# An encoder trunk on one core: pooled product after the keys, output products two gates behind, two reciprocal roots on GpSimd, first squares on ScalarE

## The chip, the core and the metric

The kernel runs on one core of a Trainium2 chip. TensorE (PE) multiplies matrices and writes to PSUM; VectorE (DVE), ScalarE (ACT) and GpSimd (POOL) do the elementwise work; SyncE (SP) issues nearly all DMAs. The metric is the device time of one execution in microseconds, taken as the median of several runs.

## The reference

Two layers of an encoder on x of 512 tokens by 1024 channels, in float32. Cut to what matters:

```python
h = rms_norm(x, attn_norm_g[l])
proj = h @ w_in[l]
c_q, c_kv, k_rope, gq, gk, gv, pool_in, gate_logits = split_columns(proj, IN_SIZES)
o_mla = mla_branch(c_q, c_kv, k_rope, ...)    # 8 heads, low rank; per-head RMS norm of q and k (96 wide), rotary part
o_gqa = gqa_branch(gq, gk, gv, ...)           # 8 heads over 2 key heads; per-head RMS norm (64 wide), rotary
o_pool = pool_branch(pool_in, pool_w[l], pool_scale[l])   # centred means over 2, 4, 8, 16 tokens minus the token, 4 linear maps
gates = sigmoid(gate_logits)                  # three branches of 1024
merged = gates0 * (o_mla @ w_branch_mla[l]) + gates1 * (o_gqa @ w_branch_gqa[l]) + gates2 * (o_pool @ w_branch_pool[l])
x = x + merged @ w_out[l]
hf = rms_norm(x, ffn_norm_g[l])
u = depthwise_conv(hf @ ffn_w_up[l], ffn_conv_w[l], ffn_conv_b[l])
x = x + (silu(u[..., :D_FF]) * u[..., D_FF:]) @ ffn_w_down[l]      # D_FF = 2816
```

## The kernel before, in words

Activations lie with channels on partitions (XM, eight chunks of 128 x 512). Every float32 operand of a product is split into a high and a low part in the fp32r format, and each product is three matmuls (`mm3`: high by high, high by low, low by high). For weights, `w_split` casts the high part on ACT (tile wh) and subtracts on DVE or POOL (tile wl); `pick` chooses which by the planner's books. Weights come in one stream of pieces (`_widths`, `_stream`, `_pack_weights`), in the order of use, over SP's queue, with three raw buffers and two pieces split ahead (LA).

The order of the instructions on every engine is written out ahead by a planner (`Clock`). It books a cost for each instruction (`Engine._count`, `_two`), and a `chain` of steps issues its next step when the last one has ended by these books. `need` and `ps` let the planner's time run on until an operand or a PSUM bank is there. On the chip the engines run these fixed queues and wait on semaphores. PSUM has two banks tagged acc, one S, two ST, two AV, one mi.

One layer goes in this order:

- Opening: the latent columns (`tok_major(latb, 384)`, eight pieces). `norm_steps` scales x and splits it into HH and HL, squares it (tile sqt) and sums the squares into sq; for the first layer, DVE squares the even chunks and ACT the odd ones, and POOL sums. `tables` makes the rotary tables (tabg, tabm) on DVE. `norm_finish` makes the reciprocal root rt and two diagonal tiles (dgh, dgl), from which PE spreads the root over partitions in `norm_rows` (rbc).
- Pool channels (`pool_steps`: windows on DVE, result split as mxh and mxl), latent turns, GQA queries (`tok_major(gqb, T)` into the banks AV, AV, mi, ST; `gq_rope` reads these banks and frees them; `gq_norm`).
- Keys and values (`tok_major(kvb, 288, pool_product)`): eight pieces, and between the fourth and the fifth `pool_product`, the four pooled products into the banks that `gq_rope` frees. Their results are split on ACT (oph) and DVE (opl), which frees the bank. `gk_evac` to `gk_norm` and `kv_evac` follow.
- Three rounds of gates, for the pool, GQA and MLA branches (br 2, 1, 0). `_order(br)` lists the units: `g` is a gate (two pieces, eight contraction steps), `b` an output product (one piece, four steps), and `q`, `n`, `v` make the MLA queries, keys and values between them. In the pool round the first two gates use the AV banks. Output product m - 1 comes behind gate m; its `product` on DVE waits for the gate's tanh on ACT and writes XM.
- The units of the pool round are filler for the GQA attention, and those of the GQA round for the MLA attention: `attention` puts scores, row maxima (`s_max`: one matmul into the S bank, then a reduction nm on DVE), probabilities (pe, ph, pl) and values at planned places, and steps the filler between them.
- `rsqrt_steps` makes a reciprocal root by a first guess y on DVE and three Newton steps of three DVE instructions each (tiles yt, y; the last one writes the root over its input). It is used for seven roots in a layer; the two 32 wide ones over ss (tile ssm) are those of the MLA queries (in `make_q`, followed by `q_norm` on MQ) and keys (in `make_n`, followed by `k_norm` on MK).
- Output projection, second norm, gated MLP with the convolution.

Of the kernel before, what the change touches and what calls it, by code (L numbers as in the profile page):

```python
# [14 lines left out]
ALU = mybir.AluOpType  # L15
# [42 lines left out]
def _order(br):  # L58


    r = []
    for m in range(KC + 1):
        r += [(k, pos.index(m)) for k, b, pos in EXTRA if b == br and m in pos]
        if m < KC:
            r.append(("g", m))
        if m > 0:
            r.append(("b", m - 1))
    return r


# [3 lines left out]

def _widths():

    r = [384] * KC + [T] * 8 + [T] * KC + [288] * 4 + [T] + [288] * 4
    for br in (2, 1, 0):
        for k, _ in _order(br):
            r += WIDTHS[k]  # L80
    return r + [T] * (2 * KC) + [T] * (4 * FC) + [T] * (2 * FC)
# [107 lines left out]
class Engine:  # L189
# [34 lines left out]
        return self.eng.tensor_reduce(out, in_, *a, **k)  # L224

    def tensor_scalar(self, out, *a):
        self._count(out, 0.00055, 0.07)
        return self.eng.tensor_scalar(out, *a)

    def tensor_copy(self, out, in_, psum=False):  # L230
# [13 lines left out]
def trunk(ctx: ExitStack, tc: tile.TileContext, x, w, prm, gb, cst, out):  # L244
# [17 lines left out]
    def slot(name, dt=F32):  # L262
        uid[0] += 1
        t = sp.tile([P, SLOT], dt, tag="s", name=f"{name}_{uid[0]}")
        return t
# [114 lines left out]
        return steps  # L380


    def norm_steps(gen, kc, g, sq, sqe=None):
        xk = XM[:, kc, :]
        hh, hl = HH[:, kc, :], HL[:, kc, :]
        t = sq if kc == 0 else slot("sqt")

        def hi():
            A.activation(hh, xk, AF.Copy, scale=g)
            if sqe is None:  # L390
                A.activation(t[:, :T], xk, AF.Square)

        def lo():
            V.scalar_tensor_tensor(hl, xk, g, f(hh), ALU.mult, ALU.subtract)
            done("H", gen, kc)

        def add():
            if sqe is not None:
                sqe.tensor_tensor(t[:, :T], xk, xk, ALU.mult)
            if kc > 0:  # L400
                G.tensor_tensor(sq[:, :T], sq[:, :T], t[:, :T], ALU.add)
            done("sq", gen, kc)

        return [hi, lo, add]

    def rsqrt_steps(a, n, key):

        y = small("y0", [P, 64])[:, :n]
        t = small("yt", [P, 64])[:, :n]

        def newton(to):
            V.tensor_tensor(t, y, a, ALU.mult)
            V.scalar_tensor_tensor(t, t, -0.5, y, ALU.mult, ALU.mult)
            V.scalar_tensor_tensor(to, t, 1.5, y, ALU.add, ALU.mult)

        def go():
            V.tensor_scalar(y.bitcast(I32), a.bitcast(I32), -0.5, RSQRT_BITS, ALU.mult, ALU.add)
            for to in (y, y, a):
                newton(to)

        return [go, lambda: done(*key)]
# [73 lines left out]
    def layer(l, sq, xsrc):  # L495
# [34 lines left out]
            chain(([("w", KC - 1), ("H", G1, KC - 1), ("sq", G1, KC - 1)], tables), after=16.0)  # L530


        def tok_major(banks, wd, between=None):
            for kc in range(KC):
                if between and kc == 4:
                    between()
                wh, wl = wnext()
                need(("H", G1, kc))
                for b in range(4):
                    bs = slice(b * P, b * P + P)  # L540
                    mm3(banks[b][:, :wd], HH[:, kc, bs], HL[:, kc, bs], wh[:, :wd], wl[:, :wd],
                        kc == 0, kc == KC - 1)
# [188 lines left out]

        ktags = ("acc", "acc", "S", "ST")
        kvb = [ps(t) for t in ktags]
        tok_major(kvb, 288, pool_product)
        gkn, kj, gk1 = slot("gkn"), slot("kj"), slot("gk1")
        krt = small("krt", [P, 4, 32], bufs=1)

# [33 lines left out]

        chain(gk_evac, gk_square, gk_sum, *rsqrt_steps(ssr[:, 32:40], 8, ("ssk", l)), ([("gkr", l)], gk_norm))
        chain(*[lambda b=b: kv_evac(b) for b in range(4)], after=2.0)

        def gk_turn():
            kT = ps("mi")
# [90 lines left out]
        def make_q(g):  # L867
            ws = (wnext(), wnext())
            st["la"] = LA - 1
            for b in range(4):  # L870
                if b:
                    yield
                bs = slice(b * P, b * P + P)
                acc = ps("acc")
                for kc, (wh, wl) in enumerate(ws):
                    need(("latT", l, kc))
                    lh, ll = lat[kc]
                    mm3(acc[:, :384], lh[:, bs], ll[:, bs], wh[:, :384], wl[:, :384], kc == 0, kc == 1)
                q_out(g, b, acc)
            st["la"] = LA  # L880
            if g == 1:
                chain(([("ssq", l, i, b) for i in range(2) for b in range(4)],
                       lambda: V.tensor_scalar(ss[:, 0], ss[:, 0], 1.0 / 96, EPS, ALU.mult, ALU.add)),
                      *rsqrt_steps(ss[:, 0].rearrange("p g b c -> p (g b c)"), 32, ("ssmq", l)),
                      *[z for i in range(2) for z in q_norm(i)])

        def q_out(g, b, acc):
# [33 lines left out]
        def make_n(g):  # L921
            wh, wl = wnext()
            need(("latT", l, 2))
            lh, ll = lat[2]
            for p in range(2):
                if p:
                    yield
                acc = ps("acc")
                two_blocks(acc, lh, ll, wh, wl, p)
                n_out(g, p, acc)  # L930
            if g == 0:
                return
            kj_ = small("kj", [P, 4, 32], bufs=1)
            kss = small("kss", [P, 4], bufs=1)

            def sums():
                V.tensor_reduce(kss, kj_, AX.X, ALU.add)
                for i in range(2):
                    V.tensor_tensor(ss[:, 1, i], ss[:, 1, i], bc(kss.unsqueeze(2), [P, 4, 4]), ALU.add)
                V.tensor_scalar(ss[:, 1], ss[:, 1], 1.0 / 96, EPS, ALU.mult, ALU.add)  # L940

            chain(lambda: V.tensor_tensor(kj_, krt, krt, ALU.mult), ([("ssn", l, i, p) for i in range(2) for p in range(2)], sums),
                  *rsqrt_steps(ss[:, 1].rearrange("p g b c -> p (g b c)"), 32, ("ssm", l)),
                  *[z for i in range(2) for z in k_norm(i)])
            chain(*rope_steps(krr, krt, tabm[:, 256:384].rearrange("p (b f) -> p b f", b=4),
                              tabm[:, 384:512].rearrange("p (b f) -> p b f", b=4), [P, 4, 32], 16, V),
                  lambda: done("krr", l))
# [437 lines left out]
        SY.dma_start(prms[l], prm[l])  # L1385
    for j in range(LA + 1):
        at(4.05 + 1.27 * j, lambda j=j: w_ahead(j))
    for kc in range(KC):
        chain(*norm_steps(0, kc, prms[0][:, PRM_AG + kc:PRM_AG + kc + 1], sq, None if kc % 2 else V),
              after=3.4 + 1.27 * kc)  # L1390
    at(30.0, lambda: V.tensor_copy(idr, ident))
    ck.to(4.3)
    for l in range(L):
# [16 lines left out]
def _pack_weights(i):  # L1410
    res = []
    for l in range(L):
        cq, ckv, kr, gq, gk, gv, pool, gate = np.split(
            i["w_in"][l], np.cumsum([256, 128, 32, 512, 128, 128, 512]), axis=1)

        def rows(*parts):
            wm = np.concatenate(parts, axis=1)
            return [wm[kc * P:kc * P + P] for kc in range(KC)]

        res += rows(cq, ckv)  # L1420
        for g in range(4):
            res += _cut(_blocks(pool[:, g * P:g * P + P], KC))
        res += rows(gq)
        res += rows(gk, gv, kr)
        res.insert(len(res) - 4, i["pool_w"][l].transpose(1, 0, 2).reshape(P, T))
        uq, ukv = i["mla_w_uq"][l], i["mla_w_ukv"][l].reshape(P, 8, P)

        wb = (i["w_branch_mla"][l], i["w_branch_gqa"][l], i["w_branch_pool"][l])
        for br in (2, 1, 0):
            for k, m in _order(br):  # L1430
                c = slice(m * P, m * P + P)
                if k == "g":
                    res += _cut(_blocks(gate[:, br * D:(br + 1) * D][:, c], KC))
                elif k == "b":
                    res += _cut(_blocks(wb[br][:, c], 4))
                elif k == "q":
                    res += [uq[kc * P:kc * P + P, m * 384:m * 384 + 384] for kc in range(2)]
                else:
                    c = slice(0, 64) if k == "n" else slice(64, P)
                    res.append(ukv[:, 4 * m:4 * m + 4, c].reshape(P, 256))  # L1440
        for m in range(KC):
            res += _cut(_blocks(i["w_out"][l][:, m * P:m * P + P], KC))
        up = i["ffn_w_up"][l]
        for c in range(FC):
            for o in (0, D_FF):
                res += _cut(_blocks(up[:, o + c * P:o + c * P + P], KC))
        dn = i["ffn_w_down"][l]
        res += _cut(np.concatenate([_blocks(dn[:, m * P:m * P + P], FC) for m in range(KC)], axis=1))
# [79 lines left out]
```

## Time and profile before

| | |
|---|---|
| time, median of 3 runs | 1695.26 us (1694.22 to 1695.61) |
| the profiled execution | 1693.48 us, of which span 1691.7 us |
| PE busy | 1649.7 us, 7360 matmuls |
| DVE, ACT, POOL busy | 946.2, 775.4, 962.6 us |
| DMA | 145.40 MB, mean 86 GB/s |
| layer 1 / layer 2 in the span | the GQA and MLA roots at about 89, 175 and 213 us / 928, 1013 and 1050 us |

The busy times of the engines overlap; a matmul's start follows the one before it by 0.23 us at 512 columns. A line of the stage view has the stretch in us, its length, the busy time and number of instructions of each engine, the granted clock of PE as a share, the share of DMA time and GB/s. A line of the wait view has the engine and the tile that it writes, then the engine and the tile that it waits for, the total in us, how often, and the longest. A line of the timeline has start, duration, engine, line, operation, tile written and tiles read, and how many were merged.

### The profile page before, as it was taken

The numbers are of one execution on the slowest core, as the hardware profiler recorded it, in microseconds if no ns is written. First come the engines' busy times: TensorE is split into PE (matmuls) and PEld (weight loads), VectorE is DVE, ScalarE is ACT, GpSimd is POOL, SyncE is SP. The second block draws the span as 40 slices with busy tenths as digits, with TensorE's granted clock in tenths as the row PEclk, the third lists the DMA queues.
The fourth block names the chain that finished last, engine by engine and source line by source line (L and its number), as shares of the span: only waits on it lengthen the run. The fifth ranks groups of instructions, "written<-read, shape, count | busy, mean of one in ns | idle before, by whom it ended". The sixth has DMA issues, their size and how long they took to land.

```text
span 1691.7 us, 20364 instructions
## 1 busy us (share of the span) xinstructions
PE 1649.7 (98%) x7360; PEld 1336.5 (79%) x7360; DVE 946.2 (56%) x1520; ACT 775.4 (46%) x1361; POOL 962.6 (57%) x759
## 2 busy tenths in 40 slices
PE   8989989999999999999999998999999999999999
PEld 7777667778888888888887786777888888888887
DVE  7776966643357666630157769666433666667100
ACT  5357645653344444432334575456434444444221
POOL 4435645764566656655544466556645665666543
PEclk9999999999999999999999999999999999999999
DMA  4221111113323232333332211111233222222331
GB/s 172 91 72 57 56 48 50 38 63 112 125 88 96 92 100 90 98 109 116 100 106 79 81 44 57 62 38 38 81 115 116 88 100 99 88 97 90 112 119 56
DMA packets 44596, 145.40 MB, mean 86 GB/s; under 512 B 5072, under 2 KB 6352, under 8 KB 44496
## 3 DMA queue, kind: packets, MB, share of 16 engines
q1 hardware_dynamic: 44352, 144.10, 25.7%
q8 instruction: 58, 0.95, 0.2%
q14 instruction: 42, 0.34, 0.1%
q10 hardware_dynamic: 144, 0.01, 0.0%
HBM read 139.90 MB, written 4.19 MB: 85 GB/s over the span
## 4 chain that ended last, share of the span: by engine, by line
PE 89%; DVE 6%; issue 2%; ACT 1%; POOL 1%; DMA 1%; SPq 0%; POOLq 0%; ACTq 0%; DVEq 0%
PE ps_acc L341 40%; PE ps_ST L341 23%; PE ps_AV L341 22%; PE ps_S L341 2%; PE ps_mi L345 1%; PE ps_mi L341 1%; DVE MQ L216 1%; POOL wl L216 1%; DVE yt L220 1%; DVE rp L216 1%; DVE nm L224 1%; DVE osum L236 0%; DVE ssm L224 0%; DVE tabg L216 0%; DMA raw<-w 0%
## 5 line engine op out<-in xcount | busy, mean ns | idle before, releaser
L216 POOL TENSOR_TENSOR wl<-raw,wh 128x512 fp32r<-128x512 f32 (+1 forms) x514 | 680.4, 1333 | 493.5 <-ACT wh L209 437.1
L209 ACT ACTIVATE wh<-raw 128x512 fp32r<-128x512 f32 (+3 forms) x522 | 313.7, 607 | 189.7 <-PE ps_ST L341 87.8
L220 DVE SCALAR_TENSOR_TENSOR a<-u,prm,a 128x512 f32<-128x512 f32 x176 | 242.3, 1377 | 79.8 <-ACT a L209 74.2
L341 PE MATMUL ps_acc<-HH,wh 128*128 128x512 f32 x592 | 236.2, 399 | 5.0 <-DVE XM L220 4.4
L341 PE MATMUL ps_acc<-HH,wl 128*128 128x512 f32 x592 | 234.9, 397 | 0.0
L341 PE MATMUL ps_acc<-HL,wh 128*128 128x512 f32 x592 | 234.9, 397 | 0.0
L216 POOL TENSOR_TENSOR pl<-pe,ph 128x512 fp32r<-128x512 f32 x109 | 143.1, 1313 | 114.2 <-ACT ph L209 77.9
L341 PEld LDWEIGHTS ps_acc<-HH,wh 128*128 128x128 f32 x592 | 112.5, 190 | 33.2 <-ACT wh L209 4.9
L341 PEld LDWEIGHTS ps_acc<-HH,wl 128*128 128x128 f32 x592 | 112.3, 190 | 26.3
L341 PEld LDWEIGHTS ps_acc<-HL,wh 128*128 128x128 f32 x592 | 112.5, 190 | 25.4
L209 ACT ACTIVATE pe<-ps_ST 128x512 f32<-128x512 f32 x128 | 76.1, 594 | 115.9 <-PE ps_ST L341 114.4
L224 DVE TENSOR_REDUCE nm<-ps_S 128x1 fp32r<-128x512 f32 x128 | 87.8, 686 | 55.5 <-PE ps_S L341 55.2
L341 PE MATMUL ps_AV<-HH,wh 128*128 128x512 f32 x288 | 113.8, 395 | 0.0
L341 PE MATMUL ps_AV<-HH,wl 128*128 128x512 f32 x288 | 113.7, 395 | 0.0
L341 PE MATMUL ps_AV<-HL,wh 128*128 128x512 f32 x288 | 113.7, 395 | 0.0
L216 POOL TENSOR_TENSOR al<-a,ah 128x512 fp32r<-128x512 f32 x44 | 58.1, 1321 | 84.8 <-ACT ah L209 58.5
L341 PE MATMUL ps_ST<-HH,wh 128*128 128x512 f32 x240 | 94.9, 395 | 0.0
L341 PE MATMUL ps_ST<-HH,wl 128*128 128x512 f32 x240 | 94.8, 395 | 0.0
L341 PE MATMUL ps_ST<-HL,wh 128*128 128x512 f32 x240 | 94.7, 395 | 0.0
L209 ACT ACTIVATE a<-u,prm 128x512 f32<-128x512 f32 x88 | 71.7, 815 | 27.6 <-DVE u L216 27.3
L209 ACT ACTIVATE ah<-a 128x512 fp32r<-128x512 f32 x44 | 27.8, 631 | 117.5 <-DVE u L240 112.0
L209 ACT ACTIVATE a<-a 128x512 f32<-128x512 f32 x44 | 27.8, 632 | 115.4 <-DVE u L240 115.4
(339 smaller groups left out, 3551.2 us busy)
## 6 DMA issues: line engine op xcount, KB each, us to landing
raw<-w SPq DMA_DIRECT2D x228, 512.0 KB, 3.4
raw<-w SPq DMA_DIRECT2D x13, 384.0 KB, 2.9
XM<-x SPq DMA_DIRECT2D x16, 256.0 KB, 3.8
raw<-w SPq DMA_DIRECT2D x6, 448.0 KB, 3.3
xsp<-XM SPq DMA_DIRECT2D x8, 256.0 KB, 2.0
XM<-xsp SPq DMA_DIRECT2D x8, 256.0 KB, 3.1
out<-XM SPq DMA_DIRECT2D x8, 256.0 KB, 2.4
raw<-w SPq DMA_DIRECT2D x4, 432.0 KB, 3.0
```

The source lines that it names most:

```text
L209: return self.eng.activation(out, in_, func, **k)
L216: return self.eng.tensor_tensor(out, *a)
L220: return self.eng.scalar_tensor_tensor(out, *a)
L224: return self.eng.tensor_reduce(out, in_, *a, **k)
L341: PE.matmul(o, lhsT=lhsT, rhs=rhs, start=start, stop=stop)
L345: PE.transpose(o, src, ident)
```

## The change

It does four things. The pooled product is issued after all eight key pieces and after the chains of the key columns are queued, and its weight comes behind the key pieces in the stream. In the pool round, output product m comes two gates behind its gate. The Newton steps of the two MLA roots go to POOL, where each takes four instructions, one of them a tensor_scalar, in place of three; the first guess stays on DVE, and the planner books a tensor_scalar on POOL at 0.2 us and 4.3 ns a column. For the first layer, ACT makes all eight squares at planned times of their own, and DVE sums them behind the last weight split of the opening.

```diff
 def _order(br):
-    r = []
-    for m in range(KC + 1):
+    r, lag = [], 2 if br == 2 else 1
+    for m in range(KC + lag):
         r += [(k, pos.index(m)) for k, b, pos in EXTRA if b == br and m in pos]
         if m < KC:
             r.append(("g", m))
-        if m > 0:
-            r.append(("b", m - 1))
+        if m >= lag:
+            r.append(("b", m - lag))
...
-    r = [384] * KC + [T] * 8 + [T] * KC + [288] * 4 + [T] + [288] * 4
+    r = [384] * KC + [T] * 8 + [T] * KC + [288] * KC + [T]
...
     def tensor_scalar(self, out, *a):
-        self._count(out, 0.00055, 0.07)
+        self._count(out, *((0.0043, 0.2) if self.kind == "Pool" else (0.00055, 0.07)))
...
-    def norm_steps(gen, kc, g, sq, sqe=None):
+    def norm_steps(gen, kc, g, sq):
...
-        t = sq if kc == 0 else slot("sqt")
+        t = sq if kc == 0 or sq is None else slot("sqt")
...
-            if sqe is None:
+            if sq is not None:
                 A.activation(t[:, :T], xk, AF.Square)
...
         def add():
-            if sqe is not None:
-                sqe.tensor_tensor(t[:, :T], xk, xk, ALU.mult)
             if kc > 0:
                 G.tensor_tensor(sq[:, :T], sq[:, :T], t[:, :T], ALU.add)
...
-    def rsqrt_steps(a, n, key):
+    def rsqrt_steps(a, n, key, eng=None):
...
         def newton(to):
+            if eng:
+                eng.tensor_tensor(t, y, a, ALU.mult)
+                eng.tensor_tensor(t, t, y, ALU.mult)
+                eng.tensor_scalar(t, t, -0.5, 1.5, ALU.mult, ALU.add)
+                eng.tensor_tensor(to, t, y, ALU.mult)
+                return
             V.tensor_tensor(t, y, a, ALU.mult)
...
-        def tok_major(banks, wd, between=None):
+        def tok_major(banks, wd):
             for kc in range(KC):
-                if between and kc == 4:
-                    between()
...
-        tok_major(kvb, 288, pool_product)
+        tok_major(kvb, 288)
...
         chain(*[lambda b=b: kv_evac(b) for b in range(4)], after=2.0)
+        pool_product()
...
-                      *rsqrt_steps(ss[:, 0].rearrange("p g b c -> p (g b c)"), 32, ("ssmq", l)),
+                      *rsqrt_steps(ss[:, 0].rearrange("p g b c -> p (g b c)"), 32, ("ssmq", l), G),
...
-                  *rsqrt_steps(ss[:, 1].rearrange("p g b c -> p (g b c)"), 32, ("ssm", l)),
+                  *rsqrt_steps(ss[:, 1].rearrange("p g b c -> p (g b c)"), 32, ("ssm", l), G),
...
+    def square(kc, t):
+        A.activation(t[:, :T], XM[:, kc, :], AF.Square)
+        done("sqt", kc)
+
+    def sum_up(kc, t):
+        if kc > 0:
+            V.tensor_tensor(sq[:, :T], sq[:, :T], t[:, :T], ALU.add)
+        done("sq", 0, kc)
+
+    sqt = [sq] + [slot("sqt") for _ in range(1, KC)]
     for kc in range(KC):
-        chain(*norm_steps(0, kc, prms[0][:, PRM_AG + kc:PRM_AG + kc + 1], sq, None if kc % 2 else V),
-              after=3.4 + 1.27 * kc)
+        chain(*norm_steps(0, kc, prms[0][:, PRM_AG + kc:PRM_AG + kc + 1], None)[:2], after=3.4 + 1.27 * kc)
+        at(9.0 + 1.27 * kc, lambda kc=kc: square(kc, sqt[kc]))
+    chain(([("w", KC - 1)], lambda: None), *[([("sqt", kc)], lambda kc=kc: sum_up(kc, sqt[kc])) for kc in range(KC)],
+          after=15.0)
...
-        res.insert(len(res) - 4, i["pool_w"][l].transpose(1, 0, 2).reshape(P, T))
+        res.append(i["pool_w"][l].transpose(1, 0, 2).reshape(P, T))
```

## Prediction

> **What bounds the kernel now.** I read the page first, then PE's time by stage, then what PE waits for, then the instructions of VectorE (DVE) and GpSimd (POOL) in the stalls, and last the granted clock behind them.
>
> ```profile
> PE 1649.7 (98%) x7360; PEld 1336.5 (79%) x7360; DVE 946.2 (56%) x1520; ACT 775.4 (46%) x1361; POOL 962.6 (57%) x759
> ```
>
> PE works 98% of the span, so only its 42 us without work and the matmuls that run at a lower clock can be won. By stage (us, busy time of PE, PEld, DVE, ACT, POOL, granted clock, DMA):
>
> ```profile
> 62.00:120.00 58.00, 53.45 (x271) 45.57 (x270) 41.01 (x85) 27.46 (x57) 26.74 (x23) 0.97 0.28 91
> 120.00:174.00 54.00, 53.97 (x246) 43.26 (x246) 35.07 (x52) 36.59 (x67) 30.67 (x25) 1.00 0.14 44
> 174.00:226.00 52.00, 43.81 (x187) 32.95 (x187) 47.71 (x81) 29.15 (x54) 30.45 (x24) 0.93 0.16 52
> 370.00:868.00 498.00, 498.00 (x2175) 407.02 (x2173) 229.34 (x340) 195.74 (x321) 289.24 (x219) 1.00 0.33 103
> 1012.00:1062.00 50.00, 43.05 (x184) 33.15 (x183) 46.32 (x80) 29.33 (x54) 29.89 (x24) 0.93 0.16 50
> ```
>
> The long product stages lose nothing. PE idles 8.2 and 7.0 us where the MLA roots are made (174 to 226, and 1012 to 1062 in layer 2), with DVE 92% busy and the clock at 0.93. PE's waits name the causes (total, times, longest):
>
> ```profile
> PE ps_S L341 <- DVE nm L224: 13.0, 5, 4.2
> PE ps_acc L341 <- DVE XM L220: 4.4, 3, 2.1
> PE ps_ST L341 <- DVE gqr L216: 4.1, 2, 2.0
> PE ps_acc L341 <- DVE wl L216: 2.7, 2, 2.5
> ```
>
> The row maxima nm hold the one S bank; XM is the first output product, which holds an acc bank; gqr is the GQA rope, which holds the ST bank that the pooled product wants; wl is an opening weight split. In the longest nm wait (start us, duration), DVE:
>
> ```profile
> 212.95 0.19 DVE L216 TENSOR_TENSOR yt<-y,ssm 128x32 f32<-128x32 f32 x1
> 213.18 1.23 DVE L220 SCALAR_TENSOR_TENSOR yt<-yt,y 128x32 f32<-128x32 f32 x1
> 214.44 0.19 DVE L220 SCALAR_TENSOR_TENSOR y<-yt,y 128x32 f32<-128x32 f32 x1
> 214.67 1.17 DVE L216 TENSOR_TENSOR yt<-y,ssm 128x32 f32<-128x32 f32 x1
> 215.87 1.19 DVE L220 SCALAR_TENSOR_TENSOR yt<-yt,y 128x32 f32<-128x32 f32 x1
> ...
> 217.88 0.68 DVE L224 TENSOR_REDUCE nm<-ps_S 128x1 fp32r<-128x512 f32 x1
> ```
>
> And POOL beside it:
>
> ```profile
> 213.06 2.73 POOL L216 TENSOR_TENSOR pl<-pe,ph 128x512 fp32r<-128x512 f32 x2 [2.99 <-ACT ph L209]
> 215.76 1.25 POOL L216 TENSOR_TENSOR wl<-raw,wh 128x512 fp32r<-128x512 f32 x1
> ```
>
> Newton's nine small steps take 0.19 us each, but one that meets a running POOL instruction ends only with it, at 1.17 to 1.23 us. The nm whose scores ended at 212.5 starts at 217.88; PE stands from 214.0 to 218.6. Two stalls cost twice, by the clock behind them:
>
> ```profile
> 114.51:117.92 3.41, 3.41 (x14) 3.14 (x11) 1.34 (x2) 1.87 (x4) 0.55 (x1) 0.50 0.47 153
> 216.91:223.74 6.83, 5.12 (x12) 3.96 (x13) 4.97 (x12) 1.54 (x3) 2.08 (x3) 0.50 0.00 0
> ```
>
> Layer 2 has such half-clock stretches at 1019.04 (3.42 us) and 1056.59 (3.41 us). Half of the busy time in all four, 15.4 us, is lost: 7.7 us, 1.7 behind the XM wait and 6.0 behind nm.
>
> **First squares.** Before, DVE makes four squares (4 x 0.68) and POOL seven sums; during four of these sums, in 11.79 to 18.86, DVE's HL takes 1.77 us (0.74 elsewhere) and three wl take 4.74 (3 x 0.55 free). PE waits 2.5 us for them. After, POOL has no sums there, DVE gets seven sums (7 x 0.69 = 4.8 us) behind the last split, and ACT four more squares (4 x 0.61 = 2.4). Queued behind the squares on ACT are the casts wh and HH: 8 x (0.72 + 0.51 + 0.61) = 14.7 us from 3.7, done near 18.4, while PE's eight pieces (2.1 us each) want the last near 20; hidden. The sums end near 22, the tables (8.2 us before, 5.8 of it four tabg at 1.5 beside POOL) near 27.5, the root and diagonals 3.8 later at 31.3; PE, 2.5 us earlier, wants them at 30.5 to 31. Gain 2.5, less up to 1.0 of waiting there: 2.0 (0 to 2.5).
>
> **Pooled product behind the keys.** The waits for gqr go: 2 x 2.0 = 4.0. The key columns then finish earlier and DVE no longer idles 1.33 us at 84.6 for oph. Instead the first gates, which take the AV banks, follow directly on the pooled product; before, half of the key product (6.4 us) lay between. AV is free after ACT's oph (0.69) and DVE's opl (0.75), against 2.1 us of product that remain; but DVE is full there (25.0 of 27 us busy in 80 to 107), with the norms (0.68 to 1.77) and key rope ahead. New wait 0 to 3 us a layer; I take 1.0, since opl1 in the trace ran 4 us behind its oph and the planner now sees the bank. Net 2.0 (-2 to 4). The pooled weight comes after eight key pieces on SP's queue: no cost, no wait of PE after the start ends with a DMA.
>
> **Two gates behind.** Gate 2's wait for XM goes: 2 x 2.1 = 4.2, and 1.7 of half clock. ACT makes ka there (4 x 0.59), then gate 0's tanh, which XM needed; now q's tiles and gate 2 share the acc banks, and q's copy and square (2 x 0.49) stand behind ka: waits of 0 to 2 us a layer (mqs has 0.4 and 1.0 already). I take 0.9 each: net 4.0 (0 to 5.9). One gate tile more stays alive; no row shows a wait for slots.
>
> **Two roots on POOL.** DVE sheds nine steps a root: four roots, 4.0 us (175.46 to 179.48) or 5.0 (212.95 to 217.96) each. The first guess y stays on DVE. POOL gets twelve instructions a root: nine tensor_tensor and three tensor_scalar. POOL's two-input rows are 1.29 at 512 wide and 0.74 at 256, so 32 wide lies near 0.27; a POOL tensor_scalar is in no row, so between the 128x1 memset (0.11) and 1.29; I take 0.3, nearest to the small forms. A root is 9 x 0.27 + 3 x 0.3 = 3.3 us, ends 1.3 and 6.3. Behind its wait for y on POOL queue pl and wl: in this stretch each pl (paired in order) is ready at least 9 us before the matmul that reads it, and no wait of PE ends with POOL between 62 and 898. Without that cover each late split would stall PE by its lateness. MQ and MK are first turned at 252, 28 us after the last norm. DVE's scaling waits for POOL, though, and behind that stand nm and the q copies. At stake: nm 6.9 + 0.3 and 6.1, and 6.0 of half clock, 19.3. I leave 4 standing (DVE is still full of MQ work, and holds 0.9 + 0.3 of these waits without Newton) and charge 0.8 us a root for DVE waiting on POOL: 12.0 (-4 to 19).
>
> POOL's row has 1.29 for a two-input step of 512 where DVE's has 0.68. [...] The rows of the stall speak for the move: there DVE paid 5.0, not 1.7.
>
> **Sum.** 2.0 + 2.0 + 4.0 + 12.0 = 20.0. Every engine's order is replanned, and a new order makes small waits of its own: the present one has vml 1.8, mqs 1.3, qb 1.1, oh 0.6 and POOL's wl 2.5, 7.3 together, in places that the change does not aim at. I give back 4, about half as much again: 16.0. The profiled execution took 1693.5 (span 1691.7 and 1.8 around it), the median 1695.3; 1693.5 - 16.0 = 1677.5, and on the median's footing 1679.
>
> The clock row sets 1.7 us on the XM wait of 2.1 us. [...]
>
> **Rivals.**
> - All goes and nothing new comes: 24.0 of waits and 7.7 of clock, 31.7: 1664. Against it: DVE stays 85% full.
> - The waits only change names: AV for gqr, acc behind ka for XM, the diagonals in the opening; the roots bring half, 6. 1695.3 - 6 = 1689. For it: DVE's full stretch.
> - The change does nothing measurable: the roots' gain is spent on DVE waiting for POOL. 1695. A measurement of this kernel tells 0.2% (3.4 us) from no change.
> - Slower: DVE stands at the MQ and MK scaling until POOL, behind one pl and one wl (2.6), has done Newton at 4.1 us: 6.7 a root, 26.8, and a half clock behind each (4 x 2.0). 35 in place of 19.3, less 8.0 of the other parts: 1703. It decides once POOL's root ends over about 4.8 us behind DVE's own next work, the length that Newton has now (19.3 / 4). Against it: POOL idles 21 of 52 us there, and the planner books 2.8 us, near my 3.3.
>
> **How the numbers follow.** Forecast 0.52 (1671 to 1686), waits renamed 0.20, all gone 0.08, nothing 0.08, slower 0.12. Faster by over 0.2%: 0.52 + 0.20 + 0.08 = 0.80; same 0.08; slower 0.12. The range 1668 to 1697 leaves out the case below and most of the slower one.
>
> **What would show it.** Right: no wl wait of PE near 13; no gqr wait and a new AV wait on opl under 1.5 us behind the key product; no XM wait before gate 2; twelve POOL rows on yt a root of 0.2 to 0.4 us; nm waits near 4 in sum, clock 1.0 through 174 to 226. Wrong: nm still near 13 with a POOL wait on DVE's MQ or MK rows; PE waits on POOL wl or pl between 120 and 230; tensor_scalar on POOL over 1 us; clock 0.5 again behind the new waits.

## The result, and the profile after

The changed kernel takes 1702.67 us (median of 5 runs, 1700.55 to 1703.98), the kernel before 1695.26. The ratio is 1.0049, 95% interval 1.0038 to 1.0060: slower by about 8 us (7.4 by the medians). The forecast was 1679, and 1702.67 lies above its range of 1668 to 1697. The profiled execution took 1703.98 us, the slowest of the five, of which 1701.9 are span (before 1691.7, 10.2 less).

The busy row of the page:

```profile
PE 1661.0 (98%) x7360; PEld 1344.0 (79%) x7360; DVE 937.6 (55%) x1493; ACT 783.0 (46%) x1371; POOL 955.0 (56%) x788
```

PE makes the same 7360 matmuls, but is busy for 11.3 us longer. DVE got 8.6 us of work off. The waits of PE (total, times, longest):

```profile
PE ps_S L341 <- DVE nm L224: 10.2, 4, 3.1
PE ps_AV L341 <- DVE opl L220: 6.7, 2, 3.4
PE ps_acc L341 <- ACT mqs L209: 5.7, 6, 1.9
...
PE ps_S L341 <- DVE sq L216: 2.9, 1, 2.9
...
PE ps_mi L341 <- DVE nm L224: 1.8, 2, 1.0
PE ps_acc L341 <- DVE XM L220: 1.6, 3, 0.8
```

Every wait that the change aims at has shrunk or gone: gqr (4.1) is no longer there, wl is 0.2 (2.7), XM 1.6 (4.4), nm 12.0 (13.3). But opl, mqs and sq stand in their places, and all waits of PE together come to 36.8 us, as against 37.6 before. So in these two traces the waits changed names at equal length, and the 10.2 us are the clock. Four of the nine stretches of half speed (stretch, length, busy times, granted clock, DMA share, GB/s):

```profile
27.52:34.35 6.83, 6.55 (x19) 5.51 (x20) 6.32 (x31) 1.78 (x6) 0.00 (x0) 0.50 0.26 78
99.20:102.61 3.41, 3.41 (x10) 2.63 (x9) 3.27 (x10) 0.52 (x1) 1.24 (x2) 0.50 0.39 149
222.08:228.91 6.83, 5.81 (x14) 4.45 (x15) 5.57 (x8) 0.94 (x2) 3.92 (x3) 0.50 0.21 55
938.88:945.71 6.83, 5.90 (x14) 4.70 (x15) 6.51 (x19) 2.00 (x7) 3.15 (x3) 0.50 0.22 78
```

They begin late in the wait for sq, in or just behind the two for opl, and in one for nm. In sum there are 41.0 us at half clock, before 17.1 (the last 2 us of the span left out). In these stretches a matmul's start follows the one before it by 0.43 us at 512 columns, where it is 0.23 at full clock; half of the difference is 12.0, near the 11.3 that PE is longer busy. Apart from the first load, both kernels have nine single stalls of 2 us or more (from one matmul's start to the next, less its own time). Before, four of them led to half clock, the two of over 4 us and two of 2.1 to 2.3; in the change all nine did, five of them of 3.1 to 3.6 us and four of 2.1 to 2.2. The other runs of the change had mean clocks of 0.988 to 0.991, this one 0.987, so part of that is chance; the runs of the kernel before had 0.992 to 0.996.

### The profile page after: what moved, and what is told of

It reads as the page before. It is cut to its first block, busy times and chain, and to the rows that moved or that the text cites. A ratio compares the mean times of both kernels' runs of the same rounds, so it can differ in the third digit from the quotient of the medians.

```text
span 1701.9 us, 20358 instructions
## 1 busy us (share of the span) xinstructions
PE 1661.0 (98%) x7360; PEld 1344.0 (79%) x7360; DVE 937.6 (55%) x1493; ACT 783.0 (46%) x1371; POOL 955.0 (56%) x788
## 4 chain that ended last, share of the span: by engine, by line
PE 88%; DVE 7%; ACT 2%; issue 1%; POOL 1%; DMA 1%; SPq 0%; POOLq 0%; ACTq 0%; DVEq 0%
PE ps_acc L341 39%; PE ps_AV L341 23%; PE ps_ST L341 22%; PE ps_S L341 2%; PE ps_mi L341 1%; PE ps_mi L345 1%; DVE gqr L216 1%; DVE rp L216 1%; DVE MQ L216 1%; DMA raw<-w 1%; DVE sq L216 1%; DVE nm L224 0%; DVE MK L216 0%; POOL yt L216 0%; POOL wl L216 0%
## 5 line engine op out<-in xcount | busy, mean ns | idle before, releaser
L216 POOL TENSOR_TENSOR wl<-raw,wh 128x512 fp32r<-128x512 f32 (+2 forms) x514 | 682.8, 1337 | 541.5 <-ACT wh L209 473.5
L216 POOL TENSOR_TENSOR pl<-pe,ph 128x512 fp32r<-128x512 f32 x97 | 129.6, 1338 | 87.9 <-ACT ph L209 55.1
```

The source lines that it names most:

```text
L216: return self.eng.tensor_tensor(out, *a)
```

## The experiments

All ratios are to the kernel before on the same chip, run beside them. Its median was 1694.86 us beside the four parts, 1694.79 beside no_lag, newt_book, lag_first and lag_rev, 1692.74 beside dve_late, after_book, book_p6 and book_p6_sq, and 1694.83 beside nolag_book, lag_book and lag_q3; runs of different groups are therefore compared by their ratios. "Waits" is the sum of PE's waits and "half clock" the sum of stretches at 0.50, both of the profiled execution.

| run | median us | ratio (95%) | waits | half clock |
|---|---|---|---|---|
| before | 1695.26 | | 37.6 | 17.1 |
| the change | 1702.67 | 1.0049 (1.0038 to 1.0060) | 36.8 | 41.0 |
| only_sq | 1692.75 | 0.9994 (0.9985 to 1.0003) | 34.0 | 30.7 |
| only_pool | 1697.35 | 1.0019 (1.0010 to 1.0028) | 36.8 | 27.3 |
| only_lag | 1703.29 | 1.0065 (1.0045 to 1.0085) | 43.6 | 20.5 |
| only_newt | 1692.75 | 0.9990 (0.9981 to 1.0000) | 35.4 | 10.2 |
| no_lag | 1693.95 | 0.9996 (0.9987 to 1.0005) | 34.9 | 17.1 |
| newt_book | 1681.72 | 0.9923 (0.9909 to 0.9936) | 30.2 | 3.4 |
| dve_late | 1692.77 | 0.9997 (0.9988 to 1.0005) | 34.5 | 23.9 |
| after_book | 1693.24 | 1.0000 (0.9990 to 1.0009) | 35.5 | 17.1 |
| nolag_book | 1685.36 | 0.9944 (0.9931 to 0.9956) | 29.7 | 17.1 |
| lag_book | 1689.71 | 0.9973 (0.9964 to 0.9983) | 34.3 | 13.7 |
| lag_first | 1705.50 | 1.0058 (1.0040 to 1.0076) | 42.0 | 27.3 |
| lag_rev | 1703.92 | 1.0057 (1.0039 to 1.0075) | 41.1 | 23.9 |
| lag_q3 | 1707.85 | 1.0075 (1.0062 to 1.0089) | 43.8 | 30.7 |
| book_p6 | 1678.72 | 0.9912 (0.9898 to 0.9926) | 27.1 | 3.4 |
| book_p6_sq | 1677.91 | 0.9908 (0.9894 to 0.9922) | 25.0 | 13.7 |

**The four parts, each alone** (A first squares, B pooled product, C two gates behind, D roots on POOL; each is its own hunks of the diff on the kernel before).

> Only the first squares go to ACT and their sums to DVE. Theory P: the wl wait of 2.5 goes, PE waits about 2.9 for sq before the first root with half clock behind it, and the waits of 2.4 before 62 go: within 2 us of before, 1693 to 1697. Theory C: no wait for sq, 1690 to 1693.

> Only the pooled product goes behind the keys. Theory P (each part trades its wait for a longer one): gqr waits 4.1 gone, AV waits on opl of about 3 a layer with half clock behind them: 1696 to 1701. Theory C: AV waits under 1 a layer, 1690 to 1693.

> Only the output products of the pool round go two gates behind. Theory P: XM waits 4.4 gone, mqs waits (1.3 before) grow to about 5, 1693 to 1698. Theory C: mqs stays under 3, 1689 to 1692.

> Only the two MLA roots go to POOL. Theory P (the root on POOL makes DVE wait and puts POOL's held splits against DVE's two-input steps): slower than before by 2 to 8 us, 1697 to 1703, DVE waits of 1.3 to 1.6 us for POOL's ssm at four places, nm waits about 10 in sum. Theory C (the roots gain as forecast, and only the four parts together go wrong): 1683 to 1691, nm waits under 6.

Against the 1694.86 of the kernel before beside them, A is 2.1 us less, B 2.5 more, C 8.4 more and D 2.1 less: 6.7 together, near the 7.4 between the medians of the change and before. By the ratios the four come to 0.0068 and the change to 0.0049, where C's interval alone is 0.002 to either side. So the parts add up within the noise, and C makes the loss. In C alone it is mostly waits, 43.6 against 37.6, with little more half clock than before (20.5 against 17.1). B is told apart from no change by its interval, and follows the theory that a part trades its wait for a longer one; A is not told apart, and D's interval ends at 1.0000. The other three expectations missed in part: A shows theory P's wait for sq (2.6) and theory C's time; C shows theory P's mqs waits (5.5) and a time 5 us above its range; D lies between its two theories, in time and in nm waits (7.1).

**The change without C, without and with the roots booked in full.** The second adds the edit of the next experiment.

> The change without its part C: the first squares, the pooled product behind the keys and the two roots on Pool are in, the output products stay one gate behind. Theory L (the order of the output products costs the attention stage some 8 us, and the rest of the change is worth a few): 1691 to 1696 us, not slower than before, the nm waits fall from 15.1 with part C alone to under 8 and the stretch from the first smax to the MQ turn takes under 132 us in both layers. Theory K (the loss comes from how the parts meet, whichever they are): 1698 to 1703, as with all four.

> The change without C and with the full booking: squares, pooled product and roots. Sum of the single runs (1681.7 for the roots booked in full, 2.5 for the pooled product behind the keys, less 2 for the squares): 1681 to 1685. If the parts also cost by meeting each other: 1688 to 1694, like the whole change with the booking.

Without C the time is that of before (1693.95), as the first theory wanted, with nm waits of 7.0. With the booking it is 1685.36, 0.4 above the range that the sum of the single runs gave and below that of the rival. By the ratios the three parts come to 0.9936 and the run to 0.9944, so meeting costs them nothing that can be told from noise.

**Part D with the root booked as long as it is.** POOL's root in the change (timeline: start, duration):

```profile
214.58 0.26 POOL L216 TENSOR_TENSOR yt<-y,ssm 128x32 f32<-128x32 f32 x1 [2.68 <-DVE y L228]
214.92 0.25 POOL L216 TENSOR_TENSOR yt<-yt,y 128x32 f32<-128x32 f32 x1
215.26 0.76 POOL L228 TENSOR_SCALAR yt<-yt 128x32 f32<-128x32 f32 x1
216.10 0.25 POOL L216 TENSOR_TENSOR y<-yt,y 128x32 f32<-128x32 f32 x1
...
218.72 0.26 POOL L216 TENSOR_TENSOR ssm<-yt,y 128x32 f32<-128x32 f32 x1
218.93 2.96 POOL L216 TENSOR_TENSOR pl<-pe,ph 128x512 fp32r<-128x512 f32 x2
221.86 1.71 POOL L216 TENSOR_TENSOR wl<-raw,wh 128x512 fp32r<-128x512 f32 x1
```

It lasts from 214.58 to 218.98, 4.4 us, where the planner books 2.8. DVE meanwhile:

```profile
219.01 1.77 DVE L216 TENSOR_TENSOR MK<-krr,ssm 128x512 f32<-128x512 f32 x1 [1.59 <-POOL ssm L216]
220.70 1.74 DVE L216 TENSOR_TENSOR MK<-MK,ssm 128x512 f32<-128x512 f32 x1
222.37 0.68 DVE L224 TENSOR_REDUCE nm<-ps_S 128x1 fp32r<-128x512 f32 x1
```

DVE stands 1.59 us for the root. Then POOL takes up the pl and wl that queued behind it, and DVE's scalings run beside those at 1.77 and 1.74, where MK steps of this size took a mean of 0.68 before:

```profile
L216 DVE TENSOR_TENSOR MK<-krr,ssm 128x512 f32<-128x512 f32 x4 | 2.7, 685 | 0.0
```

The nm on which PE waits starts only behind both, at 222.37. The experiment takes part D and books 1.7 us more for a root, 0.57 for each Newton step:

```diff
                 eng.tensor_tensor(to, t, y, ALU.mult)
+                ck.took("Pool", 0.57)
                 return
```

> Part D alone, with 0.57 us more booked on Pool for each of its three steps, so that the planner takes a root for 4.5 us, as measured, in place of 2.8. Theory N (DVE stands at the MQ and MK scalings only because the planner thinks the root done 1.7 us early and puts the scalings too far ahead): DVE's waits for Pool's ssm fall from 1.5 to under 0.5 each, and the time is 1688 to 1691.5. Rival (the later scalings push the nm steps behind them by as much, or Pool's cost moves splits to DVE): 1692 to 1697.

The time is 1681.72, 11 us under D alone and 6 below the range of the theory. DVE waits for ssm no more: in layer 1 it does three nm and three pl while POOL makes the MK root (210.71 to 215.34), and the first scaling starts at 215.81. In D alone the waits were

```profile
DVE MK L216 <- POOL ssm L216: 6.3, 2, 3.1
...
DVE MQ L216 <- POOL ssm L216: 1.7, 2, 0.9
```

and PE's nm waits fall to 1.4 (7.1 in D alone, 13.3 before):

```profile
PE ps_acc L341 <- DVE XM L220: 10.5, 6, 2.5
...
PE ps_mi L341 <- DVE nm L224: 0.9, 2, 0.4
...
PE ps_S L341 <- DVE nm L224: 0.5, 2, 0.2
```

XM waits have grown to 10.5, but no stretch in the stage of the roots drops to half clock any more:

```profile
172.00:224.00 52.00, 47.64 (x213) 36.32 (x212) 47.98 (x71) 35.18 (x66) 34.42 (x43) 1.00 0.17 56
```

In the change, 174 to 226 has 199 matmuls and a clock of 0.93; here 213 start in as long a stretch.

**Is it POOL's help, or only the later place of the scalings?** The roots stay on DVE, and the planner counts each as done 3.5 us later (`late` is 3.5 for these two roots, 0 for the others):

```diff
             for to in (y, y, a):
                 newton(to)
+            ck.fin += late
```

> The kernel before, roots on DVE as they were, but in the planner each of the two roots counts as done 3.5 us later, which puts the MQ and MK scalings behind them about as late as in part D with the full booking. Theory E (what the run with 0.57 us booked more gained, 13 us against before, comes from DVE's freed root time): no gain, 1693 to 1699. Theory O (it comes from the order alone: DVE's nm steps stand ahead of the scalings once those are put later): 1680 to 1686, with the nm waits gone as there (13.0 before, 1.4 there).

No gain: 1692.77, where the kernel before took 1692.74 beside it. The nm waits shrink to 9.3, but XM's grow to 9.1. Later scalings alone only move DVE's lateness; the gain needs the root off DVE's queue and the scalings behind the root's true end.

**The whole change with the booking** (the same added line).

> The whole change, with 0.57 us more booked on Pool for each step of the two roots. If the booking is what the change lacked: 1688 to 1693, since part C and the longer AV wait and square sums stay but the nm and mqs waits of the attention stage shrink. If part C costs its 8 us whatever DVE does: 1688 to 1691 as the sum of the single runs (1681.7 with the booking, 8 for C, 2 for the pooled product, less for the squares). If the booking helps only the order that it was tried with: 1697 to 1704.

1693.24, just above the range of the first theory. The ratio is 1.0000 in place of 1.0049, which is 8.3 us. DVE's waits for POOL's ssm are 0.9 in sum (6.1 in the change), half clock is 17.1 us instead of 41.0. The booking was one of two large faults, and with it mended the change is only level with before: C, opl and sq still cost what D wins.

**Why C loses.** Two orders that return to one gate behind, so that q1, n0 and n1 keep their places. The order of the units before, and in lag_first:

```diff
-g0 g1 b0 q0 g2 b1 g3 b2 g4 b3 q1 ...
+g0 g1 q0 g2 b0 b1 g3 b2 g4 b3 q1 ...
```

In lag_rev it is g0 g1 q0 g2 b0 g3 b1 g4 b2 b3 q1.

> The kernel before with only output product 0 two gates behind (g0 g1 q0 g2 b0 b1 g3 b2 and on as before); from gate 3 on the order is that of before, so q1, n0 and n1 come after as many units as before. Theory S (part C loses because the later q and n units come four matmul groups earlier against the attention's own steps, and DVE is late with their norms): 1690 to 1696, the XM wait of 2.3 per layer gone or shorter, the nm waits within 2 us of before's. Theory G (part C loses at gate 2 itself, the q0 products following at once and waiting for ScalarE's squares in place of the XM wait): 1697 to 1703, with 5 us of mqs waits.

> The kernel before with output products 0 to 2 two gates behind and back to one before q1 (g0 g1 q0 g2 b0 g3 b1 g4 b2 b3 q1 g5 b4 and on as before). The units ahead of q1, n0 and n1 are as many as before. Theory S (the shift of q1, n0 and n1 is what costs): 1690 to 1697, the stretch from the first smax to the MQ turn near before's 132 us. Theory G (the two-gate distance itself costs, by what waits at q0 and by the spare slots and banks): 1699 to 1704 as with the whole of part C, the stretch near 138.

Both lose as C does (lag_first 2.5 us above the range of theory G, lag_rev within its own), with mqs waits of 4.8, so the theory of the shifted q and n units falls. What the two share with C is that q0 follows gate 1 at once; they are not rid of XM's waits, though (5.5 and 4.1). PE there in only_lag:

```profile
107.46 0.60 PE L345 MATMUL ps_mi<-C,gk 128*128 128x128 f32 x4
107.82 0.42 PE L341 MATMUL ps_acc<-wh,cth 128*128 128x384 f32 x1
...
109.91 0.44 PE L341 MATMUL ps_acc<-wl,cth 128*128 128x384 f32 x1 [0.64 <-POOL wl L216]
...
113.33 0.45 PE L341 MATMUL ps_acc<-wh,cth 128*128 128x384 f32 x1 [1.68 <-ACT mqs L209]
...
118.66 0.45 PE L341 MATMUL ps_acc<-wh,cth 128*128 128x384 f32 x1 [0.80 <-ACT mqs L209]
```

And before, gate 2 behind q0:

```profile
113.58 0.47 PE L341 MATMUL ps_acc<-HH,wh 128*128 128x512 f32 x1 [2.13 <-DVE XM L220]
```

Before, the twelve matmuls of output product 0 (2.8 us) lay between the gk turn and q0. Without them q0's second piece isn't split yet (0.64 on POOL's wl), and its second product waits 1.68 us for a bank, until ACT, which copies ka up to 112.10, has squared the first. XM's 2.13 us is gone, and these come instead. With q0 one gate later:

```diff
-EXTRA = (("q", 2, (2, 5)), ("n", 2, (6, 7)), ("v", 1, (0, 3)))
+EXTRA = (("q", 2, (3, 5)), ("n", 2, (6, 7)), ("v", 1, (0, 3)))
```

> Part C alone, with the four products of q0 one gate later (g0 g1 g2 b0 q0 g3 b1 and on). Theory B (in C, q0's four products share the one accumulator bank that gate 2 leaves, right after gate 1, and so wait for ScalarE's squares; that wait is what XM's became): mqs waits about 5.5 with C, stay over 4 here since gate 3 holds a bank as gate 2 did, and the time is 1699 to 1705. Theory M (what hurts is that q0 comes ahead of output product 0, when ScalarE still evacuates the pooled and the key products): mqs waits under 2.5, 1692 to 1698.

```profile
PE ps_S L341 <- DVE nm L224: 15.5, 9, 3.0
PE ps_mi L341 <- DVE nm L224: 7.3, 3, 3.5
...
PE ps_acc L341 <- ACT mqs L209: 2.4, 2, 1.2
```

The mqs waits do fall to 2.4, so q0's place makes them; the time is nevertheless the worst, 1707.85, with nm waits of 22.8. Neither theory had that. DVE's share of the attention's splits does not explain it: 28 pl for 25.7 us, against 29 for 22.8 in only_lag (19 for 16.8 before). So q0's place explains the mqs waits, not the whole price of C, and why DVE is later still with nm here stays open.

> Parts C and D together, with the full booking, without the squares' part and the pooled product's. Theory R (C has a price of its own that D cannot take away: the XM wait of gate 2 turns into waits for q0's squares, and the order behind it is worse): 1688 to 1692, some 8 us over the 1681.7 of D with the full booking. Theory V (C was dear only because DVE was short, and with the roots off DVE it costs nothing or gains the 4 us it was meant to): 1677 to 1684.

With the roots off DVE, C still costs 8 us: 1689.71 against 1681.72, the ratios 0.9973 and 0.9923 with intervals apart. Here DVE's splits are no reason, since newt_book has 31 pl on DVE and lag_book 33. Waits are 4.1 us longer: mqs by 3.5 (1.9 to 5.4), nm by 2.7, PE's wait for wh by 2.5, and new ones of 3.5 for ACT's ph and 1.6 for POOL's wl, less 9.8 of XM and smaller ones. Half clock is 10.2 us longer, of which 5.1 are lost. Together 9.2, and the spans differ by 9.1. So C has a price of its own, as theory R had it. The mqs part of it is explained above; what in the new order makes the others was not tested.

**A place for the pooled product between the two.** B's wait for gqr needs 2.0 us more ahead of the product, and the AV banks need 3.4 behind it:

```diff
-[288] * 4 + [T] + [288] * 4
+[288] * 6 + [T] + [288] * 2
-if between and kc == 4:
+if between and kc == 6:
-res.insert(len(res) - 4, ...
+res.insert(len(res) - 2, ...
```

> Part D with the full booking, and the pooled product between the sixth and seventh key pieces in place of before's fourth and fifth, or behind the eighth as in the change. Theory T (the wait only needs 2.0 us more ahead of it for gqr and 3.4 us behind it for opl; a piece takes some 2.0 us): gqr waits 4.1 to under 0.5, opl waits under 0.5, 1676 to 1679.5. Rival (the AV bank is waited for there as well, or the shift costs the order of the attention stage): 1681 to 1688.

> As the run with the full booking and the pooled product at the sixth piece, and with all eight first squares on ScalarE and their sums on Pool from 12 us on, not on DVE behind the eighth piece. Theory W (DVE is late with the eighth piece's low half because it squares and Pool's sums hold it): wl wait at 13 us under 0.6, no wait of s2 for the sums, 1.5 to 2.5 us less than without the squares' part. Rival (the sums on Pool hold DVE's low halves, or Pool's splits come late): no change within 1 us, or up to 2 us more.

gqr and opl are both gone from the waits of PE, and two of gk come, 2.4 in sum, at the key turn:

```profile
PE ps_mi L345 <- DVE gk L216: 2.4, 2, 1.2
```

1678.72 is 0.9912 of before, in the range of theory T. The spans of the two profiled executions differ by 3.4 us from newt_book's and the waits by 3.1; by the ratios it is 1.9 us, and the two intervals overlap, so the gain is not told apart. With the squares on ACT and the sums back on POOL, the wl wait at 13 us goes (2.7 to 0.2), a wait of 1.4 for sq comes, and 1677.91 is not told apart from 1678.72, as the rival had it. Both are faster than the kernel before and the changed one by far more than their intervals. Part D with its true price is what is worth keeping; the pooled product two pieces later than before takes its waits out of the trace.

## Why the prediction was wrong, by its own steps

Two steps failed above all: output products two gates behind lose time instead of winning it, and a root on POOL is longer than it was taken and booked for. Measured alone, C missed its term by 12.4 us, D by 9.9 and the pooled product by 4.5, while the first squares' 2.1 met theirs, partly by luck; less the 4 given back, that is 22.7 of the 23.7 us between forecast and result.

- **Reading of before.** It held: the nm waits at the roots were the largest thing to win, and newt_book wins 13 us by them. The half-clock stretches were counted in the gain, but not in the new waits.
- **First squares** (taken at -2.0). wl went as said, 2.5. The sums were mis-sized: seven at 0.69, done near 22, turned out as seven at a mean of 1.25, done at 27.75,

```profile
18.72 9.03 DVE L216 TENSOR_TENSOR sq<-sq,sqt 128x512 f32<-128x512 f32 x7
```

  because POOL's wl splits of 1.3 to 1.65 us run beside them from 19.3 on: the four sums that started while a split ran ended 0.55 us behind it and took 1.56 to 1.73, the other three 0.69, the same hold that the working saw in Newton's steps. The new wait came at PE's product on sq, for which PE was ready at 24.9 (2.9, with a half clock of 6.83 from its end on), not at the diagonals with at most 1.0. The tables behind the sums, which ran beside POOL before, then took 2.7 us in place of 8.2: the collision with POOL had only moved from the tables to the sums. Alone the part measured 2.1 us less, which its interval doesn't tell from nothing.
- **Pooled product** (-2.0). gqr's 4.1 went as said. The new AV wait is the mis-sized term: taken at 1.0 a layer, bounded at 3, measured 3.3 and 3.4, and a half clock behind each in the change, which the sum had not. Alone +2.5.
- **Two gates behind** (-4.0). This step failed in sign. XM did go, 4.4 to 0.7 alone. The mechanism that it named for the replacement, q's square behind ka, is there, but taken at 0.9 a layer with a bound of 2 it is about 2.1 of mqs a layer, as long as XM's was, and 1.05 of q0's weight splits in the first layer; and the order behind it cost more still (nm waits 2.6 longer and qb 2.3), of which the cause stays open. The give-back of 4 for all new orders was too small for this part alone, which lost 8.4.
- **Two roots on POOL** (-12.0). Newton's nine steps, 1.7 us at 0.19 each, had taken DVE 5.0 in the stall. The size was right for a root that the planner knows the length of, -13 in newt_book, though partly by luck: nm fell to 1.4 where 4 was left standing, and XM's waits grew by 6.1, which no term had. The term that failed is the root's length. The tensor_tensor was well taken (0.27, measured 0.25), the tensor_scalar too when free (0.3, measured 0.22), but between any two of the twelve lie 0.08 us, 0.9 a root, and single steps are held to 0.77. So 3.3 was 4.4, DVE stood 1.45 to 1.59 a root instead of 0.8, and the booking of 2.8, which the text took as an argument against the slower rival, was what let that happen. Alone -2.1.
- **The rivals.** The slower one (DVE stands at the scaling until POOL is done, 1703) names the right place and nearly the time, but only a part of the cause: DVE's stand was 1.5 a root, not 6.7, and the 6.1 us of it in the change fall to 0.9 with the booking, with 8.3 us of time. C makes a loss of the same size. So the nearness of 1703 to 1702.67 is luck. "The waits only change names" describes the wait table exactly, 37.6 to 36.8, yet it was priced at 1689: it had the roots still bring 6, where nm fell by 1.3, and it had no term for the clock behind the renamed waits.

On the clock, the trace drops to half speed behind waits of about 2 us here too: 99.20 follows the opl wait of 3.4, but 116.27 follows the mqs stall of 2.1 and 187.94 an nm stall of 2.1. The starts at 27.52, 99.20, 116.27 and 187.94 lie 71.68, 17.07 and 71.68 us apart, which is 21, 5 and 21 times 3.413.

## What to carry to other kernels

When work moves to another engine under a planned order, measure its real length there, gaps between instructions included, and book that: the same move was worth 2 us with the root booked 1.6 short, and 13 us with it booked in full. A wait that ends with a freed bank can be cover for the next producer (here mqs waits came in XM's place); before taking it out, ask what the next user of that bank waits for, and size that from the rows. And price a stall with the clock behind it: in the two profiled executions 36.8 us of waits cost 10 us more than 37.6 had.

## What the runs showed of the hardware

- In the change, a POOL step of 128x32 that met no pl split on DVE took 0.25 us with two inputs and 0.22 us as a tensor_scalar, with 0.08 us between dependent ones. Steps that met one took 0.61 to 0.77 us (in layer 1 at 179.91, 181.92 and 215.26).
- Stretches of half clock start a whole number of steps of 3.413 us from one another within before and within the change. From the span's start, the steps lie at 1.87 us in before and at 0.21 us in the change, and on from there. All seven stalls of 3 us or more in these two were followed by a stretch; of those of 2.0 to 2.7 us, all four in the change, but two of seven before (behind the stalls that begin at 111.12 and 1015.85, not behind those at 86.21 and 925.01).
- Laid on these steps, PE was idle for 0.56 or more of the step ahead of each of the 13 stretches of before and the change, and for 0.55 or less of every other step at full clock between the first load and the last 6 us of the span. In these two traces the two kinds lie next to each other (0.56 ahead of the stretch at 116.27, 0.55 in before from 12.11 on, with none behind it), so they set no border for other kernels.
- Executions of the change differ by their clock: 1700.55 us at a mean clock of 0.991, 1703.98 at 0.987, with the three between in order.
